# Turning q and k as float32 values, splitting them behind the turn, and scaling q on ScalarE

## The chip, the cores and the metric

The kernel runs on one core of a Trainium2 chip. The metric is the device time of one execution in microseconds, the median of several runs. The engines that matter here are TensorE (PE, which does matmuls and transposes), VectorE (DVE), ScalarE (ACT), and GpSimd (POOL). PE reads its operands from SBUF and writes to PSUM; DVE and ACT read both memories. A PSUM tile called `sm` is 128 partitions of 512 float32 values, and there are four of them; one called `big` has 1024 values on each partition, and there are two.

## The reference

One encoder layer over 1024 tokens of width 1024: a half feed-forward step, attention beside a state-space scan (SSD), a second half feed-forward step and a gated embedding, with a layer norm behind each. The change touches what makes q and k for the attention. Cut to that:

```python
u = x @ w_in[i]
q, k, v, z, xs, bm, cm, dt_raw = jnp.split(u, SPLIT_POINTS, axis=-1)
qf = _rms(q.reshape(B, S, N_Q_HEADS, HEAD_DIM).astype(jnp.float32), q_norm[i])   # 8 heads of 64
kf = _rms(k.reshape(B, S, N_KV_HEADS, HEAD_DIM).astype(jnp.float32), k_norm[i])  # 2 heads of 64
qh = _apply_rope(qf, cos, sin).astype(x.dtype)
kh = _apply_rope(kf, cos, sin).astype(x.dtype)
vh = v.reshape(B, S, N_KV_HEADS, HEAD_DIM)
att_out = _block_attention(qh, kh, vh)      # softmax(q k^T / 8) v, 128 queries at a time
xbc = jnp.concatenate([xs, bm, cm], axis=-1)  # goes through a convolution, then the scan
```

`_rms` divides each head by the root of its mean square and multiplies by a weight; `_apply_rope` turns pairs of values by an angle that depends on the token. All results are float32.

## The kernel before, in words

Each product of two float32 matrices is made of three matmuls of a rounded format (`mm3`, matmul at L122): a value is split into a rounded part `hi`, a cast on ACT (L108 for weights), and the rest `lo` = value - hi, a subtraction on DVE (L87), and hi x lo, lo x hi and hi x hi are summed in PSUM.

The stage of the change is `qkv_part` (from L824). Tokens lie on partitions, 128 in a tile, 8 tiles. It first makes q: for each tile, `qq` runs 24 matmuls of 512 columns into an `sm` tile. Then it makes k, v and dt: for each tile, `kv` runs 24 matmuls of 272 columns. What follows a tile's matmuls is spread over the next steps of the loop by `step`:

- front: ACT squares the tile out of PSUM (`sq`, L848); DVE sums each head (L850) and scales the sum (L851); POOL raises it to the power -1/2 (`qr`, L853). For a k/v tile DVE also makes dt (L875) and ACT and DVE split v (L878, L87).
- back, one step later: DVE refines the root with a Newton step (L129 to L132), multiplies the tile by it out of PSUM (`qn`, L860), and does the rope: two products with the sine table (L866, into the square's tile), one with the cosine table (L867), and their sum (L868). ACT casts the sum to hi (L903 for q, L886 for k, into `qs`), and a step later DVE makes lo (L87), so that each head has hi and lo side by side, 128 columns.
- turn: PE transposes each head's 128 x 128 block of hi and lo at once. A q tile takes eight transposes into a `big` tile (L909) and one wide copy on ACT into `Q` (L910), where hi lies on the upper 64 partitions and lo on the lower 64 for each head. A k tile is laid out twice in `qs`, hi and lo each twice, and takes four transposes into an `sm` tile (L892) and a copy into `K` (L893).

The turn of a tile waits in the list `late`: `step` takes the oldest entry when more than `keep` lie there, so it follows the matmuls of a later tile. `keep` is 1 in the q loop and 2 in the k/v loop. The two tables of k are made by DVE behind k/v tile 0 (L842). What is left after the last k/v tile goes into `self.pend`, and `xbc_gemm` of the first column block of xs, B and C (x0) pops two of its entries behind each of its halves. The convolution (L972 on ACT, L977 on DVE) reads x0 out of its `big` tile; the next column block (x1) has its own.

PE's instructions are held in program order. The order on the other engines is set by a scheduler that places each instruction by its dependencies. A tile of a pool is given out again only when its last reader is done: `qwork` has two buffers of `sq` and `qn` and four of `qs`.

Of the kernel before, what the change touches and what calls it, by code (L numbers as in the profile page):

```python
# [9 lines left out]
F32 = mybir.dt.float32  # L10
F32R = mybir.dt.float32r
BF16 = mybir.dt.bfloat16
AF = mybir.ActivationFunctionType
ALU = mybir.AluOpType
# [4 lines left out]
P = 128  # L19
S = 1024  # L20
D = 1024
NT = S // P
# [4 lines left out]
HD = 64  # L27
NQ = 8
NKV = 2
# [7 lines left out]
class Layer:  # L37
# [786 lines left out]
    def qkv_part(self, c, xT):  # L824
        nc, tc, I = self.nc, self.tc, self.I
        Q, K, V = self.qkv
        tabs = c.enter_context(tc.tile_pool(name="tabs", bufs=1))
        wk = c.enter_context(tc.tile_pool(name="qwork", bufs=2))
# [7 lines left out]
        def tables(nm, scale):  # L836
            w = self.bcast(tabs, f"w_{nm}", f"{nm}n", HD)
            ws = self.bcast(tabs, f"ws_{nm}", f"{nm}ns", HD)
            T1 = tabs.tile([P, NT, HD], F32, name="T1")
            T2 = tabs.tile([P, NT, HD], F32, name="T2")  # L840
            for t_, a, b in ((T1, cs, w), (T2, sn, ws)):
                nc.vector.scalar_tensor_tensor(out=t_, in0=a, scalar=scale, in1=b.unsqueeze(1).broadcast_to([P, NT, HD]), op0=ALU.mult, op1=ALU.mult)  # L842
            T[nm] = (T1, T2)
# [9 lines left out]
            nc.gpsimd.tensor_tensor(out=r, in0=ss, in1=self.mhalf[:, :nh], op=ALU.pow)  # L853
            return v, nh, sq, ss, r

        def rope(v, nh, m, ss, r, nm, t):

            self.newton(r, ss, nh)
            qn = wk.tile([P, nh, HD], F32, name="qn")
            nc.vector.tensor_tensor(out=qn, in0=v, in1=r.unsqueeze(2).broadcast_to([P, nh, HD]), op=ALU.mult)  # L860
            T1, T2 = (x[:, t] for x in T[nm])
            H2 = HD // 2
            for a in range(2):
                o = slice(a * H2, (a + 1) * H2)
                i = slice((1 - a) * H2, (2 - a) * H2)
                nc.vector.tensor_tensor(out=m[:, :, o], in0=qn[:, :, i], in1=T2[:, o].unsqueeze(1).broadcast_to([P, nh, H2]), op=ALU.mult)  # L866
            nc.vector.tensor_tensor(out=qn, in0=qn, in1=T1.unsqueeze(1).broadcast_to([P, nh, HD]), op=ALU.mult)  # L867
            nc.vector.tensor_tensor(out=qn, in0=qn, in1=m, op=ALU.add)  # L868
            return qn

        NK = NKV * HD
        late = []

        def kv_front(t, ps):
            nc.vector.tensor_tensor(out=self.dt[:, t], in0=ps[:, 256:272], in1=dtb, op=ALU.add)  # L875
# [3 lines left out]
            self.lo(V[:, t, :, 1], vv, V[:, t, :, 0])  # L879
            return st  # L880

        def kv_back(t, st):

            kn = rope(*st, "k", t).unsqueeze(2).broadcast_to([P, NKV, 2, HD])
            kd = wk.tile([P, NKV, 2, 2, HD], F32R, name="qs", bufs=4)
            nc.scalar.copy(out=kd[:, :, 0], in_=kn)  # L886

            def turn():
                pt = self.pss().rearrange("p (g j t) -> p g j t", g=NKV, j=2)
                for g in range(NKV):  # L890
                    for j in range(2):
                        nc.tensor.transpose(out=pt[:, g, j], in_=kd[:, g, j].rearrange("p a d -> p (a d)").bitcast(F32), identity=self.ident)  # L892
                nc.scalar.copy(out=K[:, :, :, t * P:(t + 1) * P], in_=pt)  # L893
            late.append(turn)
            return kd[:, :, 1], kn, kd[:, :, 0]

        def q_front(t, ps):
            return norm(ps, NQ)

        def q_back(t, st):  # L900
            qs = wk.tile([P, NQ, 2, HD], F32R, name="qs", bufs=4)
            qn = rope(*st, "q", t)
            nc.scalar.copy(out=qs[:, :, 0], in_=qn)  # L903

            def turn():
                pt = self.psb().rearrange("p (h t) -> p h t", t=P)
                qv = qs.bitcast(F32)
                for hh in range(NQ):
                    nc.tensor.transpose(out=pt[:, hh], in_=qv[:, hh].rearrange("p a d -> p (a d)"), identity=self.ident)  # L909
                nc.scalar.copy(out=Q[:, :, t * P:(t + 1) * P], in_=pt)  # L910
            late.append(turn)
            return qs[:, :, 1], qn, qs[:, :, 0]

        backs, los = [], []

        def step(t, ps, front, back, keep=1):


            if len(late) > keep or not front:
                late.pop(0)()  # L920
            st = front(t, ps) if front else None
            if los:
                self.lo(*los.pop())
            if backs:
                los.append(backs.pop()())
            if front:
                backs.append(lambda: back(t, st))

        tables("q", HD ** -0.5)
        for t in range(NT):  # L930
            ps = self.qq(t, xT)
            if t >= NT - 2:
                self.kv_weights(t - NT + 2)
            step(t, ps, q_front, q_back)
        for t in range(NT):
            ps = self.kv(t, xT)
            step(t, ps, kv_front, kv_back, 2)
            if t == 0:
                tables("k", 1.0)
        self.pend += [lambda: step(NT, None, None, None)] * 4  # L940
        self.x0 = self.xbc_gemm(0, xT, 1)
        assert not late and not backs and not los

# [1031 lines left out]
```

## Time and profile before

| what | value |
|---|---|
| median of 3 runs | 1952.08 us (1951.97 to 1953.29) |
| the profiled execution | 1952.0 us, span 1950.2 us |
| PE busy | 1927.4 us, 99% of the span |
| DVE busy | 1526.2 us, 78% |
| ACT busy | 880.9 us, 45% |
| POOL busy | 416.0 us, 21% |
| q tiles | PE from about 699 to 747 us |
| k/v tiles | about 747 to 775 us |
| x0, the first xbc block | about 775 to 788 us |

The span is the time from the first to the last instruction of the profile; 1.8 us of the execution lie outside it. In the rows of the profile, L12 is line 12 of the kernel, `out<-in` are the program's names, and `128x512` is partitions by elements. A busy time of matmuls that are pipelined counts their overlap once, so the step from one to the next is read from the chain or from a count over a stretch, not from the duration of one.

### The profile page before, as it was taken

What the parts mean: (1) busy time and instruction counts of PE and PEld (TensorE: products, weight loads), DVE (VectorE), ACT (ScalarE), POOL (GpSimd) and SP (SyncE); (2) the same over time, 40 slices, a digit from 0 to 9 for tenths busy, and PEclk for the clock granted to TensorE, in tenths of its full rate; (3) what the DMA queues carried; (4) which work ended last, traced back from release to release, by engine and by line L of the source; (5) the groups of instructions that cost most, each with busy time, mean ns of one, the idle gap of its engine ahead of it and who ended that gap; (6) DMA issues with size and microseconds to landing.
All of it is one profiled execution on the core that took longest, in us unless ns stands there. A gap on an engine that the chain in (4) does not pass through costs nothing.

```text
span 1950.2 us, 25647 instructions
## 1 busy us (share of the span) xinstructions
PE 1927.4 (99%) x9132; PEld 1607.7 (82%) x9132; DVE 1526.2 (78%) x2364; ACT 880.9 (45%) x1509; POOL 416.0 (21%) x310
## 2 busy tenths in 40 slices
PE   8999999999999999999999999999999999999998
PEld 7888888888888889888888788888888888888886
DVE  7977777867678658758998878997686777877698
ACT  6433333325444224537887775733333333443311
POOL 0144545430001032001221001013544440001011
PEclk9999999999999999999999999999999999999999
DMA  8434554549866111231002383244545439986122
GB/s 301 138 125 154 191 179 151 194 164 373 294 221 208 61 38 59 82 120 61 6 1 88 132 290 114 92 161 163 189 155 185 163 129 354 334 262 225 33 76 98
DMA packets 147713, 310.34 MB, mean 159 GB/s; under 512 B 18128, under 2 KB 30800, under 8 KB 147584
## 3 DMA queue, kind: packets, MB, share of 16 engines
q1 hardware_dynamic: 147584, 308.69, 45.2%
q8 instruction: 72, 1.18, 0.3%
q14 instruction: 57, 0.47, 0.1%
HBM read 217.21 MB, written 91.42 MB: 158 GB/s over the span
## 4 chain that ended last, share of the span: by engine, by line
PE 95%; DVE 3%; ACT 1%; issue 0%; DMA 0%; POOL 0%; DVEq 0%; SPq 0%; ACTq 0%
PE sm L122 59%; PE big L516 12%; PE sm L516 9%; PE big L122 3%; PE big L1159 3%; PE sm L1181 2%; PE sm L1196 1%; PE sm L1197 1%; PE sm L1270 1%; PE sm L1371 1%; DVE nm L1166 1%; DVE conv L977 1%; PE sm L1281 0%; PE big L1677 0%; PE big L224 0%
## 5 line engine op out<-in xcount | busy, mean ns | idle before, releaser
L122 PE MATMUL sm<-xh,blk 128*128 128x512 f32 x1424 | 439.9, 389 | 0.0
L122 PEld LDWEIGHTS sm<-xh,blk 128*128 128x128 f32 x1424 | 267.3, 188 | 55.4
L122 PE MATMUL sm<-xl,blk 128*128 128x512 f32 x736 | 283.8, 389 | 0.0
L122 PE MATMUL sm<-blk,xl 128*128 128x512 f32 (+2 forms) x784 | 238.1, 371 | 0.2 <-ACT xn_t L1010 0.2
L122 PE MATMUL sm<-blk,xh 128*128 128x512 f32 (+2 forms) x584 | 202.7, 378 | 0.4 <-DVE accr L1464 0.4
L108 ACT CAST blk<-raw 128x512 fp32r<-128x512 f32 (+1 forms) x168 | 101.1, 610 | 214.6 <-PE sm L122 132.0
L87 DVE TENSOR_TENSOR blk<-s,blk 128x512 fp32r<-128x512 f32 x176 | 150.1, 857 | 38.3 <-ACT blk L108 36.5
L87 DVE TENSOR_TENSOR blk<-raw,blk 128x512 fp32r<-128x512 f32 (+1 forms) x168 | 144.9, 866 | 38.4 <-ACT blk L108 37.6
L108 ACT CAST blk<-s 128x512 fp32r<-128x512 f32 x172 | 105.8, 622 | 145.1 <-PE sm L122 114.7
L122 PEld LDWEIGHTS sm<-blk,xl 128*128 128x128 f32 x784 | 142.8, 188 | 24.2 <-ACT xn_t L1010 0.5
L122 PEld LDWEIGHTS sm<-xl,blk 128*128 128x128 f32 x736 | 138.1, 188 | 28.7
L178 POOL TENSOR_TENSOR ln_k<-ln_k,mhalf 128x1 f32<-128x1 f32 x32 | 36.6, 1149 | 583.3 <-DVE ln_k L177 578.3
L516 PE MATMUL big<-xh 128*128 128x512 f32 x576 | 138.8, 390 | 0.0
L267 POOL TENSOR_TENSOR s<-raw 128x512 f32<-128x512 f32 x34 | 55.1, 1620 | 384.4 <-DVE blk L87 378.2
L87 DVE TENSOR_TENSOR xh<-blk,xh 128x1024 fp32r<-128x1024 f32 x78 | 96.4, 1236 | 46.2 <-ACT xh L462 37.1
L462 ACT CAST xl<-blk 128x1024 fp32r<-128x1024 f32 x76 | 80.2, 1055 | 115.1 <-PE sm L516 41.4
L462 ACT CAST xh<-blk 128x1024 fp32r<-128x1024 f32 x78 | 82.3, 1055 | 106.0 <-PE big L516 49.2
L122 PEld LDWEIGHTS sm<-blk,xh 128*128 128x128 f32 x584 | 109.8, 188 | 19.9 <-DVE accr L1464 0.8
L516 PEld LDWEIGHTS big<-xh 128*128 128x128 f32 x576 | 107.8, 188 | 22.2
L87 DVE TENSOR_TENSOR xl<-blk,xl 128x1024 fp32r<-128x1024 f32 x76 | 92.6, 1219 | 41.9 <-ACT xl L462 37.2
L516 PE MATMUL big<-xl 128*128 128x512 f32 x480 | 115.7, 390 | 0.0
L122 PE MATMUL sm<-xET2h,blk 128*128 128x512 f32 x352 | 108.4, 389 | 0.0
(343 smaller groups left out, 4014.0 us busy)
## 6 DMA issues: line engine op xcount, KB each, us to landing
raw<-in_wi_dram SPq DMA_DIRECT2D x81, 512.0 KB
blk<-hS SPq DMA_DIRECT2D x154, 256.0 KB
hS<-h SPq DMA_DIRECT2D x88, 256.0 KB
wr<-in_wo_dram SPq DMA_DIRECT2D x44, 512.0 KB
blk<-wT SPq DMA_DIRECT2D x88, 256.0 KB
hS<-sg SPq DMA_DIRECT2D x66, 256.0 KB
wT<-wr SPq DMA_DIRECT2D x66, 256.0 KB
blk<-in_wo_dram SPq DMA_DIRECT2D x66, 256.0 KB
```

The lines of the kernel that those rows point to most:

```text
L87: (eng or self.nc.vector).tensor_tensor(out=out, in0=full, in1=hi.bitcast(F32), op=ALU.subtract)
L108: self.nc.scalar.copy(out=b[:, 0, :n], in_=src)
L122: self.nc.tensor.matmul(ps, lhsT=a, rhs=b, start=(i == 0), stop=(i == n - 1))
L178: nc.gpsimd.tensor_tensor(out=r, in0=v, in1=self.mhalf[:, :1], op=ALU.pow)
L267: lambda: G.tensor_tensor(out=s1, in0=a21, in1=a22, op=ALU.add),
L462: A.copy(out=b[:, :, 0], in_=r)
L516: nc.tensor.matmul(ps[q], lhsT=b[:, 0, x, cut], rhs=b[:, 1, y], start=j == i == 0, stop=j == NP - 1 and i == 2)
L977: nc.vector.scalar_tensor_tensor(out=a[:, o], in0=ps[:, o.start + d - c:o.stop + d - c], scalar=cw[:, j, tap:tap + 1], in1=a[:, o], op0=AL ...
L1159: nc.tensor.matmul(ps[:, n * 512:(n + 1) * 512], lhsT=Q[:, h, q0:q0 + P], rhs=K[:, h // 4, j, n * 512:(n + 1) * 512], start=j == 0, stop=j ...
L1166: nc.vector.tensor_reduce(out=nm, in_=ps, axis=AX.X, op=ALU.max, negate=True)
L1181: nc.tensor.transpose(out=pt[:, k], in_=pr[:, kk * P:(kk + 1) * P], identity=self.ident)
L1196: nc.tensor.matmul(po, lhsT=vw, rhs=pth[k // 4][:, k % 4], start=k == 0, stop=False)
```

## The change

The q and k tiles are no longer split before the turn. The rope's float32 result itself is transposed, and hi and lo are made out of PSUM behind it.

- q: ACT multiplies each head out of PSUM by its root, eight instructions of 128x64 with a scale per partition (L861), in place of one multiplication on DVE. The rope stays on DVE (L869 to L871). `qn` has four buffers.
- turn of q: two heads lie side by side in one 128x128 block, so a tile takes four transposes into half of a `big` tile (L881). Even heads come out on the upper 64 partitions, odd ones on the lower. ACT casts each half of the partitions into `Q` (two copies of 64x512, L884), and DVE subtracts (two of 64x512, L87); hi stays on the partitions that it comes out on, and lo is written to the other 64, so the subtraction reads and writes across partitions; odd heads have hi and lo the other way round.
- k: four tiles are collected in one `kn` tile and turned together: four transposes, two hi copies and two lo subtractions for half of the tokens. Two more copies on ACT (L915) put each half into the other 64 partitions of `K`.
- `keep` is 1 in the q loop and for k/v tiles 0 and 1, and 0 after that. The second half of k is turned behind x0: `pend` now holds the back of the last tile, an empty entry, the turn, and the lo.

```diff
@@ -853,11 +853,14 @@
             nc.gpsimd.tensor_tensor(out=r, in0=ss, in1=self.mhalf[:, :nh], op=ALU.pow)
             return v, nh, sq, ss, r
 
-        def rope(v, nh, m, ss, r, nm, t):
+        def rope(qn, v, nh, m, ss, r, nm, t):
 
             self.newton(r, ss, nh)
-            qn = wk.tile([P, nh, HD], F32, name="qn")
-            nc.vector.tensor_tensor(out=qn, in0=v, in1=r.unsqueeze(2).broadcast_to([P, nh, HD]), op=ALU.mult)
+            if nh == NQ:
+                for h in range(nh):
+                    nc.scalar.activation(out=qn[:, h], in_=v[:, h], func=AF.Identity, scale=r[:, h:h + 1])
+            else:
+                nc.vector.tensor_tensor(out=qn, in0=v, in1=r.unsqueeze(2).broadcast_to([P, nh, HD]), op=ALU.mult)
             T1, T2 = (x[:, t] for x in T[nm])
             H2 = HD // 2
             for a in range(2):
@@ -866,10 +869,26 @@
                 nc.vector.tensor_tensor(out=m[:, :, o], in0=qn[:, :, i], in1=T2[:, o].unsqueeze(1).broadcast_to([P, nh, H2]), op=ALU.mult)
             nc.vector.tensor_tensor(out=qn, in0=qn, in1=T1.unsqueeze(1).broadcast_to([P, nh, HD]), op=ALU.mult)
             nc.vector.tensor_tensor(out=qn, in0=qn, in1=m, op=ALU.add)
-            return qn
 
         NK = NKV * HD
-        late = []
+        late, backs, los = [], [], []
+        rows = [slice(r * HD, (r + 1) * HD) for r in range(2)]
+
+        def turned(blocks, hi, lo, then=None):
+
+            pt = self.psb()[:, :512]
+            for i, b in enumerate(blocks):
+                nc.tensor.transpose(out=pt[:, i * P:(i + 1) * P], in_=b, identity=self.ident)
+            src = [pt[rows[e]].rearrange("p (i t) -> p i t", t=P) for e in range(2)]
+            for e in range(2):
+                nc.scalar.copy(out=hi[e], in_=src[e])
+
+            def rest():
+                for e in range(2):
+                    self.lo(lo[e], src[e], hi[e])
+                if then:
+                    then()
+            los.append(rest)
 
         def kv_front(t, ps):
             nc.vector.tensor_tensor(out=self.dt[:, t], in0=ps[:, 256:272], in1=dtb, op=ALU.add)
@@ -879,52 +898,43 @@
             self.lo(V[:, t, :, 1], vv, V[:, t, :, 0])
             return st
 
+        kn = {}
+
         def kv_back(t, st):
 
-            kn = rope(*st, "k", t).unsqueeze(2).broadcast_to([P, NKV, 2, HD])
-            kd = wk.tile([P, NKV, 2, 2, HD], F32R, name="qs", bufs=4)
-            nc.scalar.copy(out=kd[:, :, 0], in_=kn)
-
-            def turn():
-                pt = self.pss().rearrange("p (g j t) -> p g j t", g=NKV, j=2)
-                for g in range(NKV):
-                    for j in range(2):
-                        nc.tensor.transpose(out=pt[:, g, j], in_=kd[:, g, j].rearrange("p a d -> p (a d)").bitcast(F32), identity=self.ident)
-                nc.scalar.copy(out=K[:, :, :, t * P:(t + 1) * P], in_=pt)
-            late.append(turn)
-            return kd[:, :, 1], kn, kd[:, :, 0]
+            h = t // 4
+            if t % 4 == 0:
+                kn[h] = wk.tile([P, 4, NKV, HD], F32, name="kn")
+            rope(kn[h][:, t % 4], *st, "k", t)
+            if t % 4 == 3:
+                Kv = K[:, :, :, h * 512:(h + 1) * 512]
+                hi, lo = ([Kv[rows[g], g, j].rearrange("p (i t) -> p i t", t=P) for g in range(2)] for j in range(2))
+
+                def then():
+                    for g in range(2):
+                        nc.scalar.copy(out=Kv[rows[1 - g], g], in_=Kv[rows[g], g].bitcast(F32))
+                late.append(lambda: turned([kn[h][:, i].rearrange("p g d -> p (g d)") for i in range(4)], hi, lo, then))
 
         def q_front(t, ps):
             return norm(ps, NQ)
 
         def q_back(t, st):
-            qs = wk.tile([P, NQ, 2, HD], F32R, name="qs", bufs=4)
-            qn = rope(*st, "q", t)
-            nc.scalar.copy(out=qs[:, :, 0], in_=qn)
-
-            def turn():
-                pt = self.psb().rearrange("p (h t) -> p h t", t=P)
-                qv = qs.bitcast(F32)
-                for hh in range(NQ):
-                    nc.tensor.transpose(out=pt[:, hh], in_=qv[:, hh].rearrange("p a d -> p (a d)"), identity=self.ident)
-                nc.scalar.copy(out=Q[:, :, t * P:(t + 1) * P], in_=pt)
-            late.append(turn)
-            return qs[:, :, 1], qn, qs[:, :, 0]
-
-        backs, los = [], []
+            qn = wk.tile([P, NQ, HD], F32, name="qn", bufs=4)
+            rope(qn, *st, "q", t)
+            Qv = Q.rearrange("p (i e) s -> p i e s", e=2)[:, :, :, t * P:(t + 1) * P]
+            hi, lo = ([Qv[rows[e ^ j], :, e] for e in range(2)] for j in range(2))
+            late.append(lambda: turned([qn[:, 2 * i:2 * i + 2].rearrange("p h d -> p (h d)") for i in range(4)], hi, lo))
 
         def step(t, ps, front, back, keep=1):
 
-
-            if len(late) > keep or not front:
+            if len(late) > keep:
                 late.pop(0)()
-            st = front(t, ps) if front else None
+            st = front(t, ps)
             if los:
-                self.lo(*los.pop())
+                los.pop()()
             if backs:
-                los.append(backs.pop()())
-            if front:
-                backs.append(lambda: back(t, st))
+                backs.pop()()
+            backs.append(lambda: back(t, st))
 
         tables("q", HD ** -0.5)
         for t in range(NT):
@@ -934,10 +944,10 @@
             step(t, ps, q_front, q_back)
         for t in range(NT):
             ps = self.kv(t, xT)
-            step(t, ps, kv_front, kv_back, 2)
+            step(t, ps, kv_front, kv_back, 1 if t < 2 else 0)
             if t == 0:
                 tables("k", 1.0)
-        self.pend += [lambda: step(NT, None, None, None)] * 4
+        self.pend += [lambda: backs.pop()(), lambda: None, lambda: late.pop()(), lambda: los.pop()()]
         self.x0 = self.xbc_gemm(0, xT, 1)
         assert not late and not backs and not los
 
```

How the instructions move. On DVE, at the last q tile (the rope of tile 7: `qn`, with `sq` as scratch and `T` the tables). Before:

```order
L860 TENSOR_TENSOR qn<-sm,qr 128x512
L875 TENSOR_TENSOR dt<-sm,dtb 128x16
L129 TENSOR_TENSOR rs_t<-qr 128x2
L866 TENSOR_TENSOR sq<-qn,T_5823 128x8x32 x2
L130 TENSOR_TENSOR rs_t<-rs_t,ss 128x2
L867 TENSOR_TENSOR qn<-qn,T_5822 128x512
L842 SCALAR_TENSOR_TENSOR T_6313<-sn,ws_k 128x512
L131 TENSOR_SCALAR rs_t<-rs_t 128x2
L868 TENSOR_TENSOR qn<-qn,sq 128x512
```

After:

```order
L869 TENSOR_TENSOR sq<-qn,T_5823 128x8x32 x2
L132 TENSOR_TENSOR qr<-qr,rs_t 128x2
L870 TENSOR_TENSOR qn<-qn,T_5822 128x512
L842 SCALAR_TENSOR_TENSOR T_6350<-sn,ws_k 128x512
L87 TENSOR_TENSOR Q<-big,Q 64x4x128 x2
L863 TENSOR_TENSOR kn<-sm,qr 128x128
L894 TENSOR_TENSOR dt<-sm,dtb 128x16
L871 TENSOR_TENSOR qn<-qn,sq 128x512
```

The multiplication by the root (L860) is no longer DVE's, and the two lo subtractions of the tile before now stand ahead of the rope's last addition (L871), which the turn of tile 7 needs. On ACT, around the last q tile and the first k/v tile (`blk<-raw` are casts of weights). Before:

```order
L903 CAST qs<-qn 128x8x64
L108 CAST blk<-raw 128x272 x4
L848 ACTIVATE sq<-sm 128x512
L910 CAST Q<-big 128x8x128
L108 CAST blk<-raw 128x512 x2
L903 CAST qs<-qn 128x8x64
L848 ACTIVATE sq<-sm 128x128
```

After:

```order
L861 ACTIVATE qn<-sm,qr 128x64 x8
L108 CAST blk<-raw 128x272 x4
L884 CAST Q<-big 64x4x128 x2
L108 CAST blk<-raw 128x272 x2
L848 ACTIVATE sq<-sm 128x512
L861 ACTIVATE qn<-sm,qr 128x64 x8
L108 CAST blk<-raw 128x512 x2
L884 CAST Q<-big 64x4x128 x2
L848 ACTIVATE sq<-sm 128x128
```

The eight scales stand ahead of the rope instead of a cast behind it. On PE, at the end of the stage: the last matmuls of x0 (`xh`, `xl` into `big`), the turn of k, and the first matmuls of x1. Before:

```order
L122 MATMUL big<-xl_5608,blk 128x512 x2
L892 MATMUL sm<-ident,qs 128x128 [waits Activation_49]
L892 MATMUL sm<-ident,qs 128x128 [waits DVE_49]
L892 MATMUL sm<-ident,qs 128x128 x2
L892 MATMUL sm<-ident,qs 128x128 [waits PE_49,Activation_49]
L892 MATMUL sm<-ident,qs 128x128 [waits DVE_49]
L892 MATMUL sm<-ident,qs 128x128 x2
L122 MATMUL big<-xh_5350,blk 128x512
L122 MATMUL big<-xl_5349,blk 128x512 x2
```

After:

```order
L122 MATMUL big<-xl_5608,blk 128x512 x2
L881 MATMUL big<-ident,kn 128x128 [waits DVE_49,PE_49]
L881 MATMUL big<-ident,kn 128x128 [waits DVE_49] x3
L122 MATMUL big<-xh_5350,blk 128x512 [waits DVE_49,PE_49,Activation_49]
L122 MATMUL big<-xl_5349,blk 128x512 x2
```

Half as many transposes stand there, in a `big` tile, and the first matmul of x1 now has a wait, which includes DVE; before, it had none.

## The prediction, made before the changed kernel was run

> **What bounds the kernel now.** I read the busy times first, then the shares of the chain that ended last, then what TensorE waited for, and only then the stage that the change touches, in time order.
>
> ```profile
> PE 1927.4 (99%) x9132; PEld 1607.7 (82%) x9132; DVE 1526.2 (78%) x2364; ACT 880.9 (45%) x1509; POOL 416.0 (21%) x310
> PE 95%; DVE 3%; ACT 1%; issue 0%; DMA 0%; POOL 0%; DVEq 0%; SPq 0%; ACTq 0%
> ```
>
> TensorE (PE) works for 1927.4 us of a 1950.2 us span and carries 95% of the last chain. Time falls when PE gets less to do, and rises by each wait that the change puts in front of a PE instruction. The waits of PE in the whole span:
>
> ```profile
> PE sm L122 <- DVE blk L87: 6.9, 1, 6.9
> ...
> PE sm L1270 <- ACT xs L1264: 1.7, 1, 1.7
> ...
> PE sm L1119 <- ACT xn_t L1010: 0.4, 1, 0.4
> ```
>
> The columns are the sum, the count and the longest. The 6.9 stands at the start. From 690 us, where the q work begins, PE waits once, 0.4 us at L1119. The chain through the q, k/v and first xbc work (start, us, what):
>
> ```profile
> 740.69 5.46 PE sm L122 x24
> 746.15 0.87 PE big L909 x8
> ...
> 753.98 3.02 PE sm L122 x24
> 757.00 0.87 PE big L909 x8
> 757.87 3.01 PE sm L122 x24
> 760.88 0.87 PE big L909 x8
> ...
> 764.76 0.44 PE sm L892 x4
> 765.20 3.01 PE sm L122 x24
> ...
> 775.57 5.47 PE big L122 x24
> 781.04 0.87 PE sm L892 x8
> ...
> 812.33 0.30 PE sm L1119
> ```
>
> A q tile is 24 matmuls in 5.46 us and eight transposes in 0.87; a k/v tile is 24 shorter matmuls in 3.01 and four transposes in 0.44. VectorE (DVE) has little room behind them:
>
> ```profile
> 750.00:760.00 10.00, 10.00 (x84) 10.00 (x83) 8.52 (x32) 3.94 (x8) 3.19 (x3) 1.00 0.19 57
> 760.00:770.00 10.00, 10.00 (x83) 10.00 (x83) 8.64 (x51) 5.02 (x15) 2.72 (x4) 1.00 0.00 0
> ```
>
> After the stretch's length come the busy times of PE, PEld, DVE, ACT, POOL and the granted clock, 1.00. DVE is busy 8.5 of 10 us, ACT 4 to 5. A longer chain through DVE shows quickly in the k/v stage, where a tile lasts 3.45 us instead of 5.9.
>
> **What is removed from PE.**
>
> ```profile
> L909 PE MATMUL big<-ident,qs x64: 270/272/273, 720.6 to 761.5; 128*128 128x128 f32 x64
> L892 PE MATMUL sm<-ident,qs x32: 270/272/273, 764.6 to 788.0; 128*128 128x128 f32 x32
> ```
>
> These 96 transposes become 32 for q and 8 for k. They are pipelined, so one costs its step, 0.87/8 = 0.109 us, not its 272 ns. 56 fewer are **-6.1 us**, all on the path that sets the end. If nothing waited: 1952.0 - 6.1 = 1945.9.
>
> **What the new instructions cost.** The nearest rows:
>
> ```profile
> 1075.83 2.04 ACT L1264 ACTIVATE xs<-xb,sdt 128x64 f32<-128x64 f32 x8
> 814.31 0.22 ACT L1108 ACTIVATE cd<-sm 128x64 f32<-128x64 f32 x1
> 814.43 0.35 ACT L1121 COPY FT<-sm 64x256 f32<-64x256 f32 x1
> L1264 ACT ACTIVATE xs<-xb,sdt x112: 331/336/365, 1069.9 to 1156.3; 128x64 f32<-128x64 f32 x112
> L1203 ACT COPY a_raw<-sm x16: 577/581/587, 905.6 to 1064.4; 64x512 f32<-64x512 f32 x16
> L1204 DVE TENSOR_TENSOR a_raw<-sm,a_raw x16: 672/689/695, 906.9 to 1065.0; 64x512 f32<-64x512 f32 x16
> 787.94 1.07 ACT L893 CAST K<-sm 128x512 fp32r<-128x512 f32 x2
> ```
>
> L1264 is the per-head scale's form, a scale per partition on 128x64, but out of SBUF: eight take 2.04 us, 0.24 a step. Out of PSUM and without the pointer, L1108 took 0.22 and the next started 0.12 behind it. So eight scales lie between 8 x 0.12 = 1.0 and 8 x 0.336 = 2.7 (no overlap at all); I take 2.0, since the form is the same. They replace one 128x512 multiplication of DVE, 0.6 by the steps below. The Trainium skill (ScalarE: Activation LUTs, "Rules for kernel authors") would give a multiplication to VectorE, not ScalarE; the two rows say the same, 2.0 against 0.6, so by that rule each chain below is 1.4 longer than with the multiplication on DVE.
>
> Two 64x512 hi copies take 1.07 (two steps of 128x512; L1203 has the same 581 ns on 64 partitions). Two 64x512 subtractions take 0.60 + 0.69 = 1.3, by L1204 and these steps:
>
> ```profile
> 747.02 0.75 DVE L866 TENSOR_TENSOR sq<-qn,T 128x256 f32<-128x256 f32 x2
> ...
> 748.97 0.68 DVE L87 TENSOR_TENSOR blk<-raw,blk 128x512 fp32r<-128x512 f32 x1
> 749.57 0.68 DVE L868 TENSOR_TENSOR qn<-qn,sq 128x512 f32<-128x512 f32 x1
> 750.17 0.68 DVE L87 TENSOR_TENSOR blk<-raw,blk 128x512 fp32r<-128x512 f32 x1
> ```
>
> DVE's sum per q tile is unchanged (two multiplications of 0.6 go, two subtractions come). ACT's grows from a cast and a wide copy, 0.5 + 0.9, to 2.0 + 1.0: with the square it stays under 4 of the 5.9 us of a q tile, so among the q tiles PE's matmuls hide all of it. They no longer do in the k/v stage.
>
> **New waits at q tiles 6 and 7.** Both kernels turn a tile some steps behind its matmuls; now tiles 5, 6, 7 are turned behind k/v tiles 0, 1, 2, one tile earlier than before. Before, tile 7's rope ended at 757.44 and its turn came at 760.88, 3.4 us of slack: exactly one k/v tile, which is spent. The ACT rows of that place:
>
> ```profile
> 745.26 0.74 ACT L108 CAST blk<-raw 128x272 fp32r<-128x272 f32 x2 [1.38 <-DMA raw<-in_wkv_dram]
> 746.25 0.60 ACT L848 ACTIVATE sq<-sm 128x512 f32<-128x512 f32 x1 [0.24 <-PE sm L122]
> 756.76 0.68 DVE L868 TENSOR_TENSOR qn<-qn,sq 128x512 f32<-128x512 f32 x1
> ```
>
> Turn of tile 6, counted from the end of tile 7's matmuls: turn of tile 4 0.44; on ACT in its order two hi copies 1.07, two casts 0.74, tile 7's square 0.60, the scales of tile 6 2.04, less three overlaps of 0.1: 4.6. Then DVE in its order: two products 0.75, dt 0.1, two weight subtractions 1.2, the cosine product 0.6, a Newton step 0.1, two lo of tile 5 1.2, the add 0.68: 9.2. PE has two turns and two k/v tiles, 2 x 0.44 + 2 x 3.01 = 6.9. **+2.3.**
>
> Turn of tile 7, from the end of that add, which is when turn 6 starts: the rest of tile 7's Newton steps and a dt, 0.55; eight scales 2.04; two products 0.75; a Newton step 0.1; cosine product 0.6; k's table (L842) 0.6; two lo of tile 6 1.2; a k product 0.2 and dt 0.1; the add 0.68: 6.8. PE has 0.44 + 3.01 = 3.45. **+3.3.** What is late next is k's rope behind it: its table and two lo stand in DVE's queue. The first turn of k, four tiles at once behind k/v tile 5, may wait for tile 3; nothing, or one pair of lo (1.2). I take **+0.3**.
>
> **A new wait at the second xbc matmul group.** K's second turn now lies in a 128x1024 PSUM buffer (`big`), and the built program makes the first matmul of the second group (x1) wait for that buffer, so for the second lo subtraction. Before, it had no wait there.
>
> ```profile
> 787.41 0.62 ACT L108 CAST blk<-raw 128x512 fp32r<-128x512 f32 x1 [1.73 <-PE big L122]
> ```
>
> This cast waits for x0's end (787.39) and stands ahead of the hi copies. From x0's end: cast 0.53, hi copies 1.07 and 0.1 to their end, 1.7; subtractions 1.3: 3.0. PE has four transposes, 0.44. **+2.6.** Lower bound 1.9, if the first subtraction runs beside the second copy (1.7 + 0.7 - 0.44). The two copies into the other half of the partitions (0.6 x 2 by L1203) run on ACT under x1's 10.9 us, and no one needs them before the attention. The 0.4 us at L1119 goes: PE comes there 0.44 + 2.6 - 0.87 = 2.2 later after x0's end, while the convolution ahead of it starts no later. **-0.4.**
>
> **Sum:** -6.1 + 2.3 + 3.3 + 0.3 + 2.6 - 0.4 = +2.0, against the profiled run's 1952.0 (span 1950.2 and 1.8 around it; the median is 1952.08): **1954.0 us**, so within 0.2% (3.9 us), about what a measurement of this kernel can tell from no change. With scales at 1.0 us the two q chains lose 1 us each: 1952.0. The likeliest case reaches from 1951 to 1956.
>
> **Rivals.**
>
> (1) *PE's saving arrives.* If turns 6 and 7 find their tiles ready and only x1 waits: 1952.0 - 6.1 + 2.6 - 0.4 = 1948.1; without any wait 1945.9. For it: before, PE waited nowhere here. Against it: 6.8 us of work must fit in 3.45, and the terms are measured durations. Half of the q waits gone gives 1951. Chance of faster by over 0.2%: 0.15.
>
> (2) *ACT's scales are dearer out of PSUM* (slower). At 0.336 us each without overlap a group takes 2.7, 0.7 more; groups 5, 6 and 7 follow each other through DVE, 3 x 0.7 = 2.1: 1956.1. It decides from about 0.3 a scale: between the scales of tiles 5 and 6 ACT has a square 0.5, two copies 1.0, six k/v weight casts 6 x 0.37 = 2.2 less overlaps of 0.1, and the eight scales, against PE's 5.46 + 0.44 = 5.9 us for the tile; past (5.9 - 3.5)/8 = 0.3 the weights come late as well, and a cast and its subtraction in the way of k/v tile 0 (0.37 + 0.43) make it 1957. For it: the step was measured out of SBUF only. Against it: L1108's row. Chance 0.18.
>
> (3) *The clock.* After the 6.9 us wait at the start PE did half as many matmuls in the first 3.41 us as in the next:
>
> ```profile
> 6.90:10.31 3.41, 3.41 (x8) 1.00 1.04 366
> 10.31:13.72 3.41, 3.41 (x16) 1.00 1.04 422
> ```
>
> A loss of 8 steps of 0.21, 1.7 us, though the granted clock (the 1.00) shows nothing of it. Behind the wait of 1.7 at L1270 the next matmuls run as ever:
>
> ```profile
> 1086.73 1.03 PE L1281 MATMUL sm<-xs,xb 128*128 128x256 f32 x4
> ...
> 1097.23 1.10 PE L1270 MATMUL sm<-state,bc 128*128 128x256 f32 x4 [1.67 <-ACT xs L1264]
> 1098.17 1.03 PE L1281 MATMUL sm<-xs,xb 128*128 128x256 f32 x4
> ```
>
> So the point lies between 1.7 and 6.9. If a wait of 3.3 us is long enough, the price is 1.7: 1955.7, and 1957.4 if the one at x1 does it too. The Trainium skill (TensorE: Matmul & The Clock Gate, "What's actually happening") has the gate close after an idle window of about 3.4 us, free-running; by it my 3.3 stays just under, and the 3.41 us of half speed above agree with such a window. Chance 0.12.
>
> (4) *The change doesn't free PE as it says*: no; the built program has 40 transposes. The chance is left out.
>
> **How the numbers follow.** The likeliest case 0.55, at 1954.0. Rival 1: 0.15. Rivals 2 and 3: 0.30, most of it above 1956.0. Some of what is called the likeliest case ends over 1956 and some of rivals 2 and 3 under it, about alike. Faster 0.15, same 0.56, slower 0.29. The range reaches from 1948.0 (only x1 waits) to 1958.0 (dear scales and one slow window).
>
> **What would show it.** In the changed profile: 40 transposes at 0.109; a wait of PE for DVE's last rope add (now L871) of about 2 us, split between k/v tile 0 and turn 6, and one of 3.3 behind k/v tile 2; a wait of 2.6 at x1 for the lo of K; eight scales in 2.0. If those waits are there and the time still is lower, the -6.1 was too small or a wait elsewhere went. If eight scales take 2.7, rival 2; if matmuls behind a wait stand 0.43 apart, rival 3. Wrong altogether if PE never waits at L881.

## The result, and the profile after

The changed kernel takes 1963.6 us (median of 5 runs, 1959.92 to 1966.63) against 1953.16 for the kernel before (5 runs, 1951.97 to 1954.42): a ratio of 1.0054, 95% interval 1.0043 to 1.0065. It is slower by about 10 us. The forecast was 1954.0 with a range of 1948.0 to 1958.0, and "within 0.2%" as the likeliest case. It was wrong.

The profiled execution took 1966.63 us, with a span of 1964.9 (before: 1950.2). Busy times and the shares of the last chain:

```profile
PE 1931.4 (98%) x9076; PEld 1608.2 (82%) x9076; DVE 1530.2 (78%) x2360; ACT 889.7 (45%) x1565; POOL 412.3 (21%) x310
PE 91%; DVE 4%; DMA 2%; ACT 1%; issue 1%; POOL 0%; SPq 0%; DVEq 0%; ACTq 0%; POOLq 0%
```

PE has 56 instructions fewer and is busy 4 us longer. 56 instructions at 0.109 us should have made it 6.1 us shorter; so some of its instructions must have been slower, by 10 us together. The waits of PE over the whole span (sum, count, longest, in us):

```profile
PE sm L122 <- DVE blk L87: 8.0, 2, 7.1
PE sm L1280 <- DVE state L1297: 4.5, 2, 3.1
PE big L881 <- DVE qn L871: 3.2, 1, 3.2
PE big L122 <- DVE K L87: 2.8, 1, 2.8
PE big L881 <- DVE rs_t L130: 1.8, 1, 1.8
PE big L881 <- DVE kn L871: 0.8, 1, 0.8
...
PE sm L1129 <- ACT xn_t L1020: 0.4, 1, 0.4
```

New are 0.9 at k/v tile 0 (in the first row, beside the 7.1 at the start), 1.8 ahead of the turn of q tile 6 (behind its add L871; the row names the instruction that ended then), 3.2 ahead of tile 7, 0.8 in k's second turn and 2.8 at x1: 9.5 us. Before, there was none of them. The chain through the stage (start, us, what; most of the pieces that are not PE's are left out):

```profile
752.17 0.68 DVE Q L87
...
752.87 0.70 DVE Q L87
753.57 0.02 issue
753.60 0.69 DVE qn L871
...
754.43 0.63 PE big L881 x4
755.06 3.03 PE sm L122 x24
...
761.31 0.71 PE big L881 x4
762.02 10.55 PE sm L122 x72
772.57 0.44 PE big L881 x4
...
794.21 24.41 PE big L122 x96
```

Two rows are longer than their count allows. 72 matmuls are three k/v tiles of 3.01 us, 9.0, and took 10.55. 96 matmuls of xbc (x1 and the next block) are 96 x 0.2275 = 21.84 and took 24.41. Both stand behind a wait. What the matmuls did there is seen in the granted clock (the number ahead of the last two):

```profile
755.00:760.00 5.00, 3.07 (x25) 2.85 (x23) 4.03 (x13) 2.65 (x10) 0.70 (x1) 1.00 0.01 2
760.00:765.00 5.00, 3.69 (x19) 3.72 (x20) 4.61 (x16) 2.03 (x6) 0.70 (x1) 0.67 0.00 0
...
790.00:795.00 5.00, 1.38 (x6) 0.89 (x5) 4.75 (x13) 4.16 (x6) 0.00 (x0) 0.74 0.53 132
795.00:800.00 5.00, 5.00 (x14) 3.90 (x14) 4.34 (x7) 2.66 (x5) 0.00 (x0) 0.57 0.30 121
800.00:805.00 5.00, 5.00 (x24) 4.14 (x23) 3.25 (x9) 2.35 (x2) 0.00 (x0) 1.00 0.00 0
```

From 795 to 800 us PE did 14 matmuls where it does 24 in the next 5 us. In the kernel before, the same slice has 24, at a granted clock of 1.00:

```profile
795.00:800.00 5.00, 5.00 (x24) 4.14 (x23) 4.83 (x11) 3.11 (x4) 0.00 (x0) 1.00 0.01 3
```

And one by one, in the changed kernel:

```profile
791.09 0.33 PE L881 MATMUL big<-ident,kn 128*128 128x128 f32 x1 [0.82 <-DVE kn L871]
794.21 0.77 PE L122 MATMUL big<-xh,blk 128*128 128x512 f32 x1 [2.79 <-DVE K L87]
794.77 1.05 PE L122 MATMUL big<-xl,blk 128*128 128x512 f32 x2
795.63 0.63 PE L122 MATMUL big<-xh,blk 128*128 128x512 f32 x1
796.05 1.05 PE L122 MATMUL big<-xl,blk 128*128 128x512 f32 x2
```

From 794.77 to 796.05 are three matmuls in 1.28 us, 0.43 each: half speed, and none of it is PE's own work that grew.

From the first turn of q to the matmul that waits for `xn_t` (L1119, now L1129) the stage took 820.89 - 720.89 = 100.0 us, against 812.33 - 720.79 = 91.5 before: **+8.5**. The rest of the 14.7 us between the two spans lies behind: the scan adds 5.2 and the remainder about 1. The scan's program did not change. In this execution its longest wait was 3.1 us, and half speed followed there too:

```profile
1107.33 2.04 PE L1280 MATMUL sm<-state,bc 128*128 128x256 f32 x4 [3.08 <-DVE state L1297]
1109.17 1.91 PE L1291 MATMUL sm<-xs,xb 128*128 128x256 f32 x4
```

Four matmuls of L1291 took 1.03 in the kernel before (L1281).

### The profile page after: what moved, and what is told of

Same layout as the page of the kernel before. It is cut to its first block, busy times and chain, and to the rows that moved or that the text cites. A ratio compares the mean times of both kernels' runs of the same rounds, so it can differ in the third digit from the quotient of the medians.

```text
span 1964.9 us, 25605 instructions
## 1 busy us (share of the span) xinstructions
PE 1931.4 (98%) x9076; PEld 1608.2 (82%) x9076; DVE 1530.2 (78%) x2360; ACT 889.7 (45%) x1565; POOL 412.3 (21%) x310
## 4 chain that ended last, share of the span: by engine, by line
PE 91%; DVE 4%; DMA 2%; ACT 1%; issue 1%; POOL 0%; SPq 0%; DVEq 0%; ACTq 0%; POOLq 0%
PE sm L122 55%; PE big L516 12%; PE sm L516 9%; PE big L122 3%; PE big L1169 3%; PE sm L1191 2%; PE sm L1206 1%; PE sm L1207 1%; PE sm L1280 1%; DMA wr<-in_wo_dram 1%; PE sm L1381 1%; DVE nm L1176 1%; PE sm L1291 0%; PE big L224 0%; PE sm L224 0%
## 5 line engine op out<-in xcount | busy, mean ns | idle before, releaser
L87 DVE TENSOR_TENSOR blk<-raw,blk 128x512 fp32r<-128x512 f32 (+1 forms) x168 | 148.2, 887 | 37.5 <-ACT blk L108 36.9
L87 DVE TENSOR_TENSOR blk<-s,blk 128x512 fp32r<-128x512 f32 x176 | 151.0, 863 | 31.5 <-ACT blk L108 29.8
L87 DVE TENSOR_TENSOR xh<-blk,xh 128x1024 fp32r<-128x1024 f32 x78 | 95.5, 1224 | 48.6 <-ACT xh L462 42.5
L87 DVE TENSOR_TENSOR xl<-blk,xl 128x1024 fp32r<-128x1024 f32 x76 | 92.8, 1221 | 40.8 <-ACT xl L462 33.2
```

What stands on the lines that cost most here:

```text
L87: (eng or self.nc.vector).tensor_tensor(out=out, in0=full, in1=hi.bitcast(F32), op=ALU.subtract)
```

## The experiments

Theory A, formed on this profile: the new waits cost their own length, and in addition PE falls to half speed for up to 3.4 us when it has been idle for some 3 us. The rivals: B, ACT's eight scales are the loss; C, the loss lies in the scan; D, only the place of the turns is wrong; E, turning plain float32 and splitting behind it is dear in itself. The last column but one of the table is read off each profile as the shift of the attention's first matmul against its time in the kernel before (878.0 us), the last as the shift of the first transposition of `y` at the scan's end (1146.8); executions don't reach the stage at the same time, and the shifts hold that too. Against the kernel before, the first turn of q comes 1.1 us later in the profiles of k in the other pool and of the wait of 5.1, 0.7 to 0.8 later with q scaled on DVE and in both filled kernels, 0.4 later with the k part alone, and within 0.2 in the others.

| kernel | median us, runs | before, same runs | ratio, 95% interval | shift at the attention | at the scan's end |
|---|---|---|---|---|---|
| the change | 1963.6, 5 | 1953.16 | 1.0054 (1.0043 to 1.0065) | +8.5 | +13.7 |
| q scaled on DVE | 1961.63, 4 | 1952.84 | 1.0048 (1.0032 to 1.0065) | +7.1 | +8.0 |
| later turns | 1963.04, 4 | 1952.84 | 1.0052 (1.0037 to 1.0067) | +9.8 | +10.1 |
| k in the other PSUM pool | 1958.21, 8 | 1952.84 | 1.0028 (1.0018 to 1.0039) | +3.2 | +5.8 |
| k part alone | 1951.5, 10 | 1952.84 | 0.9994 (0.9984 to 1.0003) | -1.2 | -1.0 |
| q part alone | 1957.36, 10 | 1952.95 | 1.0023 (1.0014 to 1.0033) | +4.0 | +3.8 |
| wait of 2.0 put in | 1955.32, 10 | 1952.95 | 1.0013 (1.0004 to 1.0022) | +2.5 | +2.5 |
| wait of 2.8 put in | 1956.29, 10 | 1952.95 | 1.0019 (1.0010 to 1.0028) | +4.7 | +4.7 |
| wait of 5.1 put in | 1961.67, 4 | 1952.95 | 1.0044 (1.0029 to 1.0059) | +8.2 | +8.4 |
| the change, waits filled | 1960.73, 4 | 1952.4 | 1.0042 (1.0027 to 1.0057) | +5.9 | +7.9 |
| wait of 5.1, filled | 1960.29, 5 | 1952.4 | 1.0036 (1.0024 to 1.0048) | +6.2 | +8.3 |
| k part, later preparation | 1949.95, 11 | 1952.4 | 0.9988 (0.9979 to 0.9997) | -2.6 | -2.6 |
| the same, q tiles 0 to 2 too | 1949.79, 11 | 1952.4 | 0.9985 (0.9976 to 0.9994) | -3.1 | -3.1 |

### One part of the change undone

**q scaled on DVE again.**

```diff
-            if nh == NQ:
-                for h in range(nh):
-                    nc.scalar.activation(out=qn[:, h], in_=v[:, h], func=AF.Identity, scale=r[:, h:h + 1])
-            else:
-                nc.vector.tensor_tensor(out=qn, in0=v, in1=r.unsqueeze(2)..., op=ALU.mult)
+            nc.vector.tensor_tensor(out=qn, in0=v, in1=r.unsqueeze(2)..., op=ALU.mult)
```

> The change with one part undone: q is scaled by one multiplication on DVE again, as before. Theory A (PE's new waits cost their own length, and each wait near 3 us also makes PE run at half speed for some us behind it): the eight scales of ACT stand only in the chains to turns 6 and 7; 1.64 us of scales become 0.6 of DVE, so the wait at turn 7 falls from 3.2 to about 2.1, and its half-speed stretch (about 1.5 us in the changed profile) goes with it, while the wait at x1 (2.8) and its stretch (2.6) stay. Time 1.5 to 3 us below the changed kernel, still 7 or more above the kernel before. Theory B (ACT's scales are the loss): back to the time before or under it, 1947 to 1953. Theory C (the loss lies in a later stage, in the scan): no change from the changed kernel.

Measured: 1961.63, 2.0 below the changed kernel, which lies inside the spread of the two kernels' runs, and 8.8 above the one before. Theory B falls: the scales are not the loss. The wait at turn 7 did shrink, from 3.2 to 1.0 us, more than expected, but the one at turn 6 grew from 1.8 to 4.0 (0.9 at k/v tile 0 went). The work of DVE that stands before both turns was not less, so the wait only moved. In the slice of 755 to 760 us behind it the granted clock was 0.66.

**The turns of q tiles 5 to 7 one k/v tile later.**

```diff
-            step(t, ps, kv_front, kv_back, 1 if t < 2 else 0)
+            step(t, ps, kv_front, kv_back, (2, 2, 1)[t] if t < 3 else 0)
```

> The change with the turns of q tiles 5, 6, 7 one k/v tile later, where they were before (keep 2, 2, 1, 0). Theory A: the same DVE work has to be done by the end of the stage, so the waits are not removed but cut up: about 0.8 at k/v tile 0, under 1.2 each at turn 7, at the next k/v tile's PSUM buffer and at k's first turn, 8 to 9 us in all with x1's 2.8 as in the changed kernel; none in the q and k/v stage is long enough for a half-speed stretch, so the time falls by about 1.5 only. If only the place of the turns were at fault (theory D): the 0.9, 1.8 and 3.2 us and the stretch go, 7 us off the changed kernel.

Measured: 1963.04, so nothing gained. D falls. The waits are cut up as expected (PE in this stretch):

```profile
PE big L881 <- DVE kn L871: 2.5, 2, 1.6
PE big L881 <- DVE qn L871: 1.4, 1, 1.4
PE sm L122 <- DVE kn L863: 1.0, 1, 1.0
```

But theory A was wrong on one point: I expected no half-speed stretch behind such short waits, and there were two (0.71 in the slice of 760 to 765; 0.73 in 770 to 775 and 0.59 in the next). Between the 1.4 and the 1.0 lie only the four transposes of tile 7 (0.6 us), and behind them the matmuls stood 0.23 us apart instead of 0.13. The second stretch follows waits of 1.0 and 1.6 with one transpose between them. So it is not one long wait that counts, but how idle PE was over a stretch of some 3 us.

**k turned in the other PSUM pool**, so that x1 doesn't have to wait for the buffer.

```diff
-            pt = self.psb()[:, :512]
+            pt = self.pss() if sm else self.psb()[:, :512]      # sm is true for k
```

> The change with k turned in a 512-wide PSUM tile of the other pool, so that x1's first matmul has no wait for k's lo. Theory A: x1's wait (2.8) and the half-speed stretch behind it (2.6 in the changed profile) both go: about 5.4 below the changed kernel. If a wait costs its length alone: 2.8 below. Waits at turns 6 and 7 as in the changed kernel.

Measured: 1958.21, 5.4 below the changed kernel, what theory A gave; by the wait alone it would have been 2.8. The wait at x1 is gone, and the slices from 790 to 805 us all stand at 1.00. In this execution the wait of 3.2 at turn 7 was followed by no half speed (slice 760 to 765: 1.00), though it was as long as in the changed kernel. The loss behind a wait of this length is there in some executions and in others not. So the agreement of the medians with theory A is in part luck: counted from the first turn, the stage of the profiled execution is 6.4 us shorter than the changed kernel's, since the 1.5 of half speed at turn 7 are missing too.

### The two parts apart

**k alone**: q as before, k as in the change, in the 512-wide pool.

> The kernel before with the k part of the change alone: q as before (scaled on DVE, split ahead of eight transposes), k as in the change, its turns in the 512-wide PSUM pool, keep 1 for k/v tiles 0 to 2. 24 transposes fewer are 24 x 0.109 = 2.6 us. Theory A: no wait of PE is added, so 2 to 2.6 us faster than the kernel before, and no half-speed stretch in the q, k/v and first xbc stage. If turning plain float32 and splitting behind it is itself dear (theory E): no gain.

Measured: 1951.5, 1.3 below the kernel before; the interval (0.9984 to 1.0003) just reaches 1. No new wait in the stage and no slower slice; the stage became shorter, so E falls for k; for q it isn't tested apart from the waits. About half of the expected gain went into a wait that had been 0.4:

```profile
PE sm L1133 <- ACT xn_t L1024: 1.6, 1, 1.6
```

PE comes to this place 2.3 us earlier, but the copy on ACT for which it waits starts only 1.15 earlier (810.55 against 811.70). The convolution isn't what holds it up: it starts earlier than before, at 788.87 against 790.81. But ACT now makes `ldt` for the decays, with the load of its table 1.6 us (L1099), at 807.44, between the second step of the convolution and that copy; before, the load stood at 801.48 and `ldt` at 804.50, where ACT had idle time. This is read off the two profiles, not tried by itself.

**q alone**: q as in the change with the turns where they were, k as before.

> The kernel before with the q part of the change alone (ACT's scales, turn of float32, split behind it); k is split, turned and copied as before, and the turns of q stand where they were before (keep 2). 32 transposes fewer are 3.5 us. Theory A: the longer work of ACT and DVE per q tile reaches into the k/v stage, where DVE was 85% busy; PE waits there in five to seven short pieces of 0.2 to 1.2 us, 4 to 5 us in all, so +1 us against the kernel before, and up to +4 if these pieces lie close enough together for a half-speed stretch. Theory D (only the place of the turns or k was at fault): 3.5 us faster than the kernel before.

Measured: 1957.36, 4.4 above the kernel before. The waits are 0.9, 1.5, 1.2 in two and 0.7, 4.3 us in all, in pieces of at most 1.5 where 1.2 was worked out; the slice of 760 to 765 us stands at 0.69. The q part by itself is a loss: it makes PE's work 3.5 us shorter and returns more than 4 in waits, and half speed comes on top (the first k/v tile behind the waits takes 4.60 us instead of 3.0). The other large part of the changed kernel's loss is k's PSUM buffer, the 5.4 above.

### The wait and the clock by themselves

Into the kernel before, one wait of PE is put ahead of x1. The number of squarings (1, 2, 3) sets its length; the transposed tile isn't used.

```diff
+                if j == 0:
+                    late = zwk.tile([P, 512], F32, name="late")
+                    nc.vector.tensor_copy(out=late, in_=ps[:, 512:])
+                    for _ in range(1):
+                        nc.vector.tensor_tensor(out=late, in0=late, in1=late, op=ALU.mult)
+                    nc.tensor.transpose(out=self.pss()[:, :P], in_=late[:, :P], identity=self.ident)
```

> The kernel before, with one wait of PE put in and nothing else: DVE copies part of x0 out of PSUM and squares the copy once, PE transposes it into a spare tile, ahead of x1's matmuls. The result of the transposition is not used. A wait of about 2.1 us at that place. Theory A, with a clock that looks at a stretch of about 3.4 us that starts at no fixed time: 2.1 us slower than before, in some runs up to 1.7 more. Rival (a wait costs its length): 2.1, with the spread of the kernel before.

> As the one before, with the copy squared twice: a wait of about 2.9 us. Theory A: 2.9 slower and in most runs 1 to 2 us more, with half speed seen behind the wait in the profile. Rival (a wait costs its length): 2.9.

> As the one before, with the copy squared three times, the last behind two steps of the convolution on DVE: a wait of about 5 us. Theory A: half speed behind it in every run, 5.0 + 1.7 or a little more. Rival (a wait costs its length): 5.0.

Measured, in that order: waits of 2.0, 2.8 and 5.1 us, with a transposition of 0.3 to 0.4 behind each; medians 2.4, 3.3 and 8.7 above the kernel before. The rows behind the wait, of the first:

```profile
790.42 0.30 PE L988 MATMUL sm<-ident,late 128*128 128x128 f32 x1 [1.99 <-DVE late L987]
790.48 0.47 PE L122 MATMUL big<-xh,blk 128*128 128x512 f32 x1
790.79 0.63 PE L122 MATMUL big<-xl,blk 128*128 128x512 f32 x2
791.25 0.40 PE L122 MATMUL big<-xh,blk 128*128 128x512 f32 x1
```

of the second:

```profile
791.06 0.30 PE L988 MATMUL sm<-ident,late 128*128 128x128 f32 x1 [2.79 <-DVE pm L1084]
...
792.12 0.89 PE L122 MATMUL big<-xl,blk 128*128 128x512 f32 x2
792.80 0.63 PE L122 MATMUL big<-xh,blk 128*128 128x512 f32 x1
793.23 1.06 PE L122 MATMUL big<-xl,blk 128*128 128x512 f32 x2
...
796.23 0.40 PE L122 MATMUL big<-xh,blk 128*128 128x512 f32 x1
```

and of the third:

```profile
794.51 0.42 PE L988 MATMUL sm<-ident,late 128*128 128x128 f32 x1 [5.14 <-DVE late L987]
794.58 0.78 PE L122 MATMUL big<-xh,blk 128*128 128x512 f32 x1
795.16 1.05 PE L122 MATMUL big<-xl,blk 128*128 128x512 f32 x2
```

Behind 2.0 us PE goes on at full speed (three matmuls from 790.48 to 791.25, 0.26 each). Behind 2.8 it starts at full speed and drops to half one microsecond later, for about 3.4 us: what decides seems to run by its own time, not from the wait's end. Behind 5.1 it starts at half; there the 96 matmuls of x1 and the next block take 23.31 us instead of 21.8, and the stage, counted from the first turn, is 7.1 longer, near the 6.7 expected. The price is not fixed. In the ten runs with 2.0 us, seven are 1.3 to 2.8 above the median before and three (1957.24, 1957.25, 1957.7) more than 4; with 2.8, eight are 2.0 to 4.3 above and two 6.0 and 6.4. With 5.1 all four are 6.6 to 10.6 above. My expectation "in most runs 1 to 2 more" for 2.8 us was too high: the median of that kernel is about what the wait and the transposition cost alone, and its half speed (23.44 us for the 96 matmuls) is shown by the profiled execution, not by the median.

**The same waits filled.** PE is given matmuls that nobody reads, ahead of the instructions that wait.

```diff
+        def filler(out, n):
+            x = xT[0][0][0]
+            for _ in range(n):
+                nc.tensor.matmul(out, lhsT=x[:, 0, :P], rhs=x[:, 0, :512], start=True, stop=True)
...
+            filler(whole[:, 512:], ahead)       # 6 and 13 for q tiles 6 and 7, 3 for k's second turn
             for i, b in enumerate(blocks):
                 nc.tensor.transpose(...)
+            if behind:
+                filler(self.pss(), behind)      # 11 ahead of x1
```

> The changed kernel with PE kept at work while it waits: matmuls whose result nobody reads stand ahead of the turns of q tiles 6 and 7 (6 and 13), ahead of k's second turn (3) and ahead of x1 (11), 33 of 0.2275 us, 7.5 us, all inside waits of 1.8, 3.2, 0.8 and 2.8 us. The computation is the same. Theory A (half speed follows PE's idleness): the places come no later, since the fillers fit into the waits, and the half-speed stretches of 1.5 and 2.5 us go: 3 to 6 us below the changed kernel, about 1957 to 1960, with less spread. Rival (time is lost for another reason, with the waits): no change from 1963.6, or slower by what does not fit.

> The kernel with the wait of about 5 us put in, with 20 matmuls of 0.2275 us (4.55 us, result not read) inside that wait. Theory A: the wait's own length stays (5.1 us, now mostly filled), the half-speed loss goes: 5.1 us above the kernel before instead of 8.7. Rival: 8.7 as without fillers.

Measured: the changed kernel with 33 matmuls more takes 1960.73, 2.9 less; each against the kernel before in its own runs, 8.3 above instead of 10.4, with intervals that overlap, so the median alone doesn't prove a gain. Its four runs lie within 1 us (1960.19 to 1961.08) where the changed kernel's lay 6.7 apart. The two long rows of the chain are back at their length:

```profile
762.54 9.04 PE sm L122 x72
...
793.91 22.03 PE big L122 x96
```

against 10.55 and 24.41: 3.9 us of these two rows were half speed, and this is shown by a change that only gives PE work inside its waits. The waits for DVE that are left over there are 0.9, 0.4, 0.3, 0.9 and 0.3. The gain is at the low end of the 3 to 6 expected or under it, and the profile shows two reasons. The stage, from the first turn of q to the matmul that waits for `xn_t`, took 96.7 us, 3.3 less than in the changed kernel and not 3.9: PE now comes to k's first turn 1.6 us sooner, counted from q's first turn, and waits 0.9 there for the addition of k's rope, which it didn't in the changed kernel. And the scan had a slow slice (0.83 at 1100 to 1110 us).

The kernel with 5.1 us put in and 20 fillers takes 1960.29, 7.9 above, where 5.1 was expected. In the profile its 96 matmuls behind the wait take 21.79 instead of 23.31, and no slice of the stage is slower; the shift at the attention is +6.2, of which 0.8 is a late start, so 5.4 in the stage. The scan adds 2.1, with half speed in it. The lowest of its five runs, 1956.86, is 5.2 above the lowest before; the expectation holds for that run and not for the median. So the stage answers the expectation to within 0.3 us, and in the profiled execution the scan spoils it; where the other runs lost their time isn't recorded.

### A version that is faster than both

Where PE doesn't have to wait, the fewer transposes are worth about what they should. To the k part alone, the preparation of the scan's decays was moved behind the fourth xbc block, to do away with the wait of 1.6 us:

```diff
-            if j in (0, 2):
+            if j in (0, 3):
                 next(prep, None)
```

> The kernel with the k part alone, with one thing more: the preparation of the scan's decays (the PE group that waited 1.6 us for a copy on ACT there, and 0.4 in the kernel before) stands behind the fourth column block of xbc instead of the third. Theory: the wait falls back to 0.4 or less: 1.2 us below the kernel with the k part alone, 2.5 to 3 below the kernel before.

and q tiles 0 to 2 were then made as in the change, tiles 3 to 7 as before, with `keep` at 2, 2, 2, 1 and 0 in the k/v loop:

> As the one before, and q tiles 0 to 2 as in the change (ACT's scales, four transposes, split behind), tiles 3 to 7 as before, turns of the last q tiles one k/v tile later (keep 2, 2, 2, 1, 0). 12 transposes fewer are 1.3 us. Theory: those tiles lie where DVE has room, so no wait in the q tiles; one of about 0.7 at k's first turn; 0.5 us below the one before, 3 to 3.5 below the kernel before.

Measured: 1949.95 and 1949.79, 2.5 and 2.6 below the kernel before (ratios 0.9988, 0.9979 to 0.9997, and 0.9985, 0.9976 to 0.9994). The wait at the preparation is 0.4 again. Part of the first is due to the moved preparation, which would take 0.4 or less of wait from the kernel before as well; that was not tried alone. The three q tiles are worth 0.5 in the profile (-2.6 and -3.1; 0.2 of it is an earlier start) and 0.2 in the medians, which the runs can't tell from nothing; one wait of 0.5 at k's first turn came with them.

## Why the prediction was wrong, step by step

**The bound** was right: PE sets the end, and each new wait of PE came out in the time.

**-6.1 for 56 transposes**: right in kind. Where no wait took its place, 24 fewer (the k part alone) made the stage 1.5 us shorter, counted from the first turn, beside a wait that grew by 1.2: 2.7, with 2.6 worked out.

**The prices**: the eight scales cost less than the 2.0 taken. The two copies cost 1.20 where 1.07 was taken, and the two subtractions 1.39 (from 752.17 us) where 1.3 was. ACT behind the last q tile:

```profile
747.51 1.75 ACT L861 ACTIVATE qn<-sm,qr 128x64 f32<-128x64 f32 x8
...
750.12 1.20 ACT L884 CAST Q<-big 64x512 fp32r<-64x512 f32 x2
```

A step of 0.21, out of PSUM, against 0.24 out of SBUF. Rival 2 falls with that row.

**+2.3 at turn 6, +3.3 at turn 7**: 0.9 + 1.8 = 2.7 and 3.2. The chains were as counted, down to the order of DVE's instructions. **+0.3 at k's first turn**: none in the changed kernel, and 0.9 in the filled one, where PE comes there sooner. Its place was taken by one that I had no term for, **0.8 in k's second turn**: the rope of the last k tile stands in DVE's queue behind the weight subtractions of x1, which wait for a DMA and its cast:

```profile
ACT blk L108 <- DMA raw<-in_wx_dram: 6.4, 3, 3.1
```

(ACT's waits from 695 to 830 us; the row of before was 2.5, 2, 1.5.) **+2.6 at x1**: 2.8. **-0.4 at L1119**: it stayed 0.4. I had taken it that what ACT does ahead of this matmul starts no later; but its last part, a step of the convolution, a cast and the copy, starts only when PE ends the block that the step reads (818.62 us in the changed kernel), so it moves with PE. With the two small errors the sum of the terms is -6.1 + 2.7 + 3.2 + 0.8 + 2.8 = +3.4 instead of +2.0. Each of the first transposes behind a wait takes about 0.2 more than its step (0.63, 0.71 against 0.44 for four), some 0.8 together, which I hadn't counted either.

**The step that failed is rival 3, the clock.** It was named, with a price of 1.7 for one wait and 3.4 for two, given a chance of 0.12, and left out of the sum. From this kernel's rows I had that "the point lies between 1.7 and 6.9"; I then set it near the length of one whole window, 3.4 us, so that a wait of 3.3 "stays just under". The runs show that it need not fill such a stretch: half speed came behind 2.8 in one piece, and behind 1.4 and 1.0 close together, and not behind 2.0 in the profiled execution. By that the waits that I myself worked out, 2.3 and 3.3 within 7 us and 2.6 with a transposition ahead of it, were long enough, and the likeliest case was 1954.0 + 1.4 for the terms + 0.8 + 1.5 and 2.5 of half speed, about 1960. The filled kernel shows 3.9 us of it. The measured median is 3 to 4 us above this 1960. The Trainium skill (TensorE: Matmul & The Clock Gate, "What's actually happening") names an idle window of about 3.4 us that runs free. The free running agrees with the late drop behind the 2.8 us wait and with executions that differ behind the same wait of 3.2; what I had read into the window, that a wait has to fill it, doesn't agree with half speed behind 2.8, or behind 1.4 and 1.0.

**The rest**, up to the +14.7 of the profiled execution, lies in the scan: 5.2 there. Its program is the same. The longest wait for `state` was 3.1 us in this execution, 1.6 before and 1.6 to 2.7 in the experiments, because DVE waited there 1.6 us for a store of `y` to finish (0.7 at most before). Slow slices in the scan appear in four of the fourteen profiles (the change, k in the other pool, and both filled kernels) and not in the kernel before. Why they come in these and not in others that reach the scan as late (later turns, a wait of 5.1) stays open; theory C, that the loss lies there, holds for 5.2 of the profiled execution's 14.7 and for none of the 8.5 in the stage.

**Range and chances.** 1958.0 as the upper end held one slow stretch with dear scales, not two or three slow stretches with the waits. The range was too narrow because the clock's price was set at a single loss and thought of as rare.

## What to carry to other kernels

When a change gives back TensorE's work and puts waits in its place, add up the idle time over a stretch of some 3 us, not the longest single wait. Here 2.4 us of it in two pieces, or 2.8 in one, could bring half speed, while 2.0 in one did not in the execution that was profiled. Where it came, it cost 1.5 to 2.5 us per place beside the wait, and a spread of several us between runs. Instructions that move to a less busy engine helped only where the tile's time had room: the q tiles had 5.9 us each, the k/v tiles behind them 3.45, and the same chain that was hidden in the one stood on TensorE's path in the other. And when an output buffer moves to another PSUM pool, look whose next use of that pool then waits for the last reader.

## What the runs showed of the hardware that I had not expected

Half speed set in one microsecond behind the end of a 2.8 us wait, after matmuls at full speed, and lasted about 3.4 us; a wait of 5.1 was followed by it at once. The same wait of 3.2 us at the same place was followed by it in the execution of the changed kernel and not in the one with k in the other pool. In these slices the granted clock of the profile shows it (0.57 to 0.74), while at the start of the program, where PE did 8 matmuls in 3.41 us instead of 16, it shows 1.00. And matmuls without use, put into the waits, brought the matmuls behind them back to full speed: 9.04 instead of 10.55 us, and 22.03 instead of 24.41.
